# A SwiGLU's last down projection: three pairs in seven products, pair by pair through four banks, none plainly

## The chip, the cores and the metric

One core of a Trainium2 chip runs the whole kernel. TensorE (PE in the profile) multiplies matrices into PSUM banks, VectorE (DVE) and ScalarE (ACT) do the elementwise work, GpSimd (POOL) adds a few small operations and accumulating DMAs, SyncE (SP) issues most DMAs. The metric is the device time of one execution in microseconds. Three runs of the kernel before gave 2554.17, 2554.62 and 2554.91; the median, 2554.62, stands as its time.

## The reference

Two groups of tokens (512 and 256) go through two layers with shared weights. Each layer is a half SwiGLU, a mixer, and a half SwiGLU, all on a residual stream of width 1024; a final RMSNorm ends it. Everything is float32.

```python
def swiglu(h, wg, wu, wd):
    return (jax.nn.silu(h @ wg) * (h @ wu)) @ wd

def even_layer(x, ...):
    x = x + 0.5 * swiglu(rmsnorm(x, f1_n), f1_g, f1_u, f1_d)
    x = x + mixer_ab(rmsnorm(x, mix_n), w_in, ...)
    x = x + 0.5 * swiglu(rmsnorm(x, f2_n), f2_g, f2_u, f2_d)
    return x

def odd_layer(x, ...):
    x = x + 0.5 * swiglu(rmsnorm(x, f1_n), f1_g, f1_u, f1_d)
    x = x + mixer_c(rmsnorm(x, mix_n), w_qkv, rpb, w_out)
    x = x + 0.5 * swiglu(rmsnorm(x, f2_n), f2_g, f2_u, f2_d)
    return x
```

`wg` and `wu` are 1024 x 2816, `wd` is 2816 x 1024. So there are four SwiGLUs. What follows them is, in order: the first mixer, the next layer's SwiGLU, the second mixer, and the end of the kernel.

## The kernel before

**Layout.** The residual stream lies transposed: `x[m]`, m = 0 to 7, holds 128 of the 1024 features for all 768 tokens. The tokens are cut into two halves of 384 (`H`), the free size of nearly every matmul.

**Precision.** A float32 product is made of three fp32r products. Each operand is split into a high part (a copy by ACT) and a low part (source minus high part, by DVE); `mm3` issues high x high, high x low, low x high. `wsplit` splits a 128 x 512 weight tile into `whi` and `wlo`, which come from a pool of five places each; `split` does it for operands of 384 columns.

**Seven products.** The hidden width 2816 is eleven *pairs* (`NPAIR`) of two blocks of 128. For one pair, the down projection is a 2 x 2 block product: two hidden blocks, two halves of the outputs (features of m < 4 and of m >= 4), two halves of the tokens. A scheme of Strassen's kind makes it in seven block products instead of eight. The weight operands are three of the four blocks (`a11`, `a12`, `a22`) and the sums `s1` (of two blocks), `s3` (of two blocks), `s2` = `s1` + `a11`, `s4` = `s2` + `a12`. `s1` and `s3` are built by DMA: SP loads one block, POOL issues a second DMA that accumulates onto it (`wsum`); `s2` and `s4` are DVE adds (`sums`). The operand side has `b11`, `b21`, `t1`, `t2`, `t3`, `b22`, `n4`, each a split of a hidden tile or of a difference of such tiles (`operands`, a generator that is stepped by hand). A block product covers four 128-feature blocks j, each in a PSUM bank of its own. Banks carry names: X gets b11 then b21; Y starts as a copy of X after b11 and gets t2, t3, n4; Z gets t1 then b22. Between products a bank's content is added to, or subtracted from, `x` where the scheme wants it (`add`), and `out` does the last such add for a row and then calls `final`.

**The order of pairs.** `ffn` makes gate and up projections pair by pair, with the down projection of pairs 0 to 7 two at a time in between (`down`). The last three pairs, 8, 9 and 10, come in `down_last`. There, pairs 8 and 9 go together in seven products, and pair 10, whose hidden tiles are ready last, goes *plainly*: its two blocks are two more weight tiles per output half (`quads`, split by `lasts`), and its operands are just the split hidden tiles (`operand`), four block products for each hidden block. For each j, `part` does both pairs' matmuls one after the other into the bank, then `plain` adds pair 10's.

**What follows decides the order in `down_last`.** `lag` is true before another SwiGLU and at the end, false before a mixer. With `lag`: b11, t2, b21, t3, then X finished plainly, n4 with Y finished plainly, `half_done(0)` (the norm of token half 0 may begin), t1, the plain product of the other half in a bank V, b22 finished plainly, `half_done(1)`. Without: b11, t2, b21, X finished plainly, t1, b22 finished plainly, t3, copies of Y into four further banks W, then for each j n4 and the two plain products. At the end of the kernel the last block is cut into columns (`CUTS`: 256 and 128) so that the final norm of the first part may start early.

**What `final` does** for a row m: its squares (ACT) are summed into `acc` (DVE); before a SwiGLU the row is fed into that SwiGLU's operands (`feed`); before a mixer, when the row's second half is done, the row is scaled by the norm's gain and split into `xh[m]` (ACT) and `xl[m]` (DVE), on which the mixer's first projection waits. Before the first mixer this goes in two halves of 384 columns; before the second the tokens are turned, and the parts are 448, 64 and 256 columns, so that the first spans both halves. The mixer's first projection goes through m = 0 to 7 in order.

**Order on the engines.** The program fixes the order on PE (with small matmuls of the norm put in by an own count of PE's time, `tick`). On the other engines and the DMA queues a scheduler orders the instructions when the program is built: those listed earlier go first among the ones that its model holds ready, and a later one may go ahead while an earlier one isn't. Tiles of a tag share a fixed number of places: 8 raw weight tiles (`raw`), 8 tiles for sums (`s`), 30 operand tiles of 384 columns (`e`), 5 places for `whi` and `wlo`, four PSUM banks in each of two pools (`mm`, `aux`).

## Time and profile before

| what | value |
|---|---|
| median of three runs | 2554.62 us |
| the profiled execution | 2555.03 us |
| its span in the profile | 2553.3 us |
| PE, PEld busy | 99%, 97% |
| DVE, ACT, POOL busy | 82%, 54%, 13% |
| the four runs of `down_last` (start to end on PE) | 452.30 to 498.74; 1179.08 to 1225.87; 1663.71 to 1711.13; 2494.55 to about 2544.2 |

In the profile, PE is the matmul, PEld the weight load beside it, an instruction's row names its start, its length, its engine and source line, and output <- inputs. Almost every matmul has line 191 (inside `mmul`), so stages are told apart by tile names: `db`, `dt`, `dn` are the operands b11/b21/b22, t1/t2/t3 and n4 of the paired products, `dh` those of pair 10's plain ones, `whi`/`wlo` (or `khi`/`klo`) the weights, `ps_mm` and `ps_aux` the banks, `xh`/`xl` a mixer's operands. On DVE, line 877 and 879 are `add` for m < 4 and m >= 4, 281 the norm's sum, 993 `xl`, 168 `wlo`, 745 `sums`. Idle time of an engine stands in brackets with what ended it.

### The profile page before, as it was taken

How to read it: one execution, taken by the hardware profiler on the slowest of the kernel's cores; microseconds unless marked ns; L12 is line 12 of the kernel's file. 1: busy time of each engine (PE TensorE's matmuls, PEld its weight loads, DVE VectorE, ACT ScalarE, POOL GpSimd, SP SyncE). 2: the span in 40 equal slices, each digit the busy share in tenths (PEclk: the TensorE clock that was granted, in tenths of full speed). 3: DMA queues.
4: the chain of work that ended last, by engine and by line, in shares of the span. 5: the costliest groups of instructions: out<-in, count | busy, mean ns of one | idle time of the engine just before them, and what ended most of it. 6: DMA issues, size and time to landing. Idle time of an engine off the chain costs nothing.

```text
span 2553.3 us, 42563 instructions
## 1 busy us (share of the span) xinstructions
PE 2535.2 (99%) x15160; PEld 2475.6 (97%) x15160; DVE 2092.9 (82%) x4206; ACT 1369.3 (54%) x2844; POOL 322.7 (13%) x398
## 2 busy tenths in 40 slices
PE   9999999999999999999999999999999999999998
PEld 8999999988899999999999999999999999999998
DVE  8987888888879778888988788876667598878887
ACT  7554455546665545445654445554455475444553
POOL 1110111000111111110111011112112111101100
PEclk9999999999999999999999999999999999999999
DMA  8654555431256455552665455432212256545451
GB/s 235 159 133 120 131 134 148 145 98 62 73 146 175 120 126 127 131 131 79 161 153 132 117 127 125 121 124 70 63 61 65 88 148 164 135 119 126 123 125 54
DMA packets 187156, 310.88 MB, mean 122 GB/s; under 512 B 31680, under 2 KB 46528, under 8 KB 186944
## 3 DMA queue, kind: packets, MB, share of 16 engines
q1 hardware_dynamic: 149248, 240.49, 29.4%
q0 software_dynamic: 36864, 67.13, 16.7%
q8 instruction: 119, 1.95, 0.3%
q14 instruction: 93, 0.76, 0.1%
q10 hardware_dynamic: 832, 0.55, 0.1%
HBM read 298.65 MB, written 15.07 MB: 123 GB/s over the span
## 4 chain that ended last, share of the span: by engine, by line
PE 92%; DVE 4%; ACT 1%; issue 1%; DMA 1%; POOL 0%; SPq 0%; ACTq 0%; DVEq 0%; POOLq 0%
PE ps_mm L191 60%; PE ps_aux L191 30%; PE ps_aux L202 1%; DVE wlo L168 1%; DMA s<-in_w 1%; DVE ol L255 0%; DMA raw<-in_w 0%; DVE u L587 0%; DVE s L745 0%; ACT whi L167 0%; DMA x<-in_x 0%; ACT xh L992 0%; DVE db L255 0%; DVE dt L255 0%; DVE tl L255 0%
## 5 line engine op out<-in xcount | busy, mean ns | idle before, releaser
L167 ACT CAST whi<-s 128x512 fp32r<-128x512 f32 x508 | 310.6, 620 | 384.3 <-PE ps_mm L191 198.6
L168 DVE TENSOR_TENSOR wlo<-s,whi 128x512 fp32r<-128x512 f32 x508 | 345.3, 687 | 173.6 <-ACT whi L167 152.0
L148 POOL DMA_DIRECT2D s<-in_w x256 | 223.5, 911 | 1442.0 <-DVE db L255 356.7
L167 ACT CAST whi<-rawp 128x512 fp32r<-128x512 f32 x344 | 211.4, 619 | 255.5 <-PE ps_mm L191 100.7
L168 DVE TENSOR_TENSOR wlo<-rawp,whi 128x512 fp32r<-128x512 f32 x344 | 234.4, 686 | 23.4 <-ACT whi L167 14.4
L191 PE MATMUL ps_mm<-db,whi 128*128 128x384 f32 (+1 forms) x948 | 240.2, 334 | 0.0
L191 PE MATMUL ps_aux<-dt,whi 128*128 128x384 f32 x880 | 223.3, 334 | 0.0
L191 PEld LDWEIGHTS ps_mm<-db,whi 128*128 128x128 f32 x948 | 170.8, 188 | 0.0
L191 PE MATMUL ps_mm<-db,wlo 128*128 128x384 f32 (+1 forms) x474 | 158.4, 334 | 0.7 <-DVE wlo L168 0.7
L191 PEld LDWEIGHTS ps_aux<-dt,whi 128*128 128x128 f32 x880 | 158.8, 188 | 0.0
L191 PE MATMUL ps_aux<-dt,wlo 128*128 128x384 f32 x440 | 147.2, 334 | 0.3 <-DVE wlo L168 0.3
L191 PE MATMUL ps_mm<-xh,whi 128*128 128x512 f32 (+1 forms) x416 | 144.4, 347 | 0.0
L167 ACT CAST whi<-raw 128x512 fp32r<-128x512 f32 x164 | 100.4, 619 | 79.6 <-PE ps_mm L191 56.9
L191 PE MATMUL ps_mm<-xl,whi 128*128 128x512 f32 (+1 forms) x416 | 140.2, 337 | 0.0
L191 PE MATMUL ps_mm<-xh,wlo 128*128 128x512 f32 (+1 forms) x416 | 140.1, 337 | 0.0
L168 DVE TENSOR_TENSOR wlo<-raw,whi 128x512 fp32r<-128x512 f32 x146 | 99.0, 687 | 27.2 <-ACT whi L167 25.1
L587 DVE TENSOR_TENSOR u<-ps_aux,u 128x384 f32<-128x384 f32 x176 | 97.3, 553 | 7.6 <-PE ps_aux L191 7.4
L1190 ACT ACTIVATE p<-p,st 128x256 f32<-128x256 f32 (+3 forms) x144 | 69.1, 481 | 54.9 <-DVE st L1185 54.8
L191 PEld LDWEIGHTS ps_mm<-db,wlo 128*128 128x128 f32 x474 | 89.0, 188 | 1.5 <-DVE wlo L168 1.5
L191 PEld LDWEIGHTS ps_mm<-xh,whi 128*128 128x128 f32 x416 | 78.9, 190 | 9.4 <-issue 1.2
L191 PEld LDWEIGHTS ps_mm<-xh,wlo 128*128 128x128 f32 x416 | 78.8, 189 | 8.6
L191 PEld LDWEIGHTS ps_mm<-xl,whi 128*128 128x128 f32 x416 | 79.0, 190 | 6.7
(508 smaller groups left out, 8028.2 us busy)
## 6 DMA issues: line engine op xcount, KB each, us to landing
rawp<-in_w SPq DMA_DIRECT2D x384, 256.0 KB, 3.1
s<-in_w SPq DMA_DIRECT2D x256, 256.0 KB, 2.8
s<-in_w POOLq DMA_DIRECT2D x256, 256.0 KB, 5.0
raw<-in_w SPq DMA_DIRECT2D x163, 256.0 KB, 2.9
xdm<-x SPq DMA_DIRECT2D x16, 384.0 KB, 2.3
x<-in_x SPq DMA_DIRECT2D x16, 192.0 KB, 4.8
x<-xdm SPq DMA_DIRECT2D x8, 384.0 KB, 3.8
tab<-skew SPq DMA_DIRECT2D x8, 256.0 KB, 3.6
```

The lines of the kernel that those rows point to most:

```text
L148: self.nc.gpsimd.dma_start(f, y, accum_op=ALU.add)
L167: i = nc.scalar.copy(hi, src).ins
L168: self.behind = i, (eng or nc.gpsimd).tensor_tensor(out=lo, in0=src, in1=hi.bitcast(F32), op=ALU.subtract).ins
L191: self.nc.tensor.matmul(out, lhsT=lhsT, rhs=rhs, start=start, stop=stop, **kw)
L202: self.nc.tensor.transpose(out, src, self.ident)
L587: nc.vector.tensor_tensor(out=t, in0=bank[key, n], in1=t, op=ALU.add)
L1190: nc.scalar.activation(outs[i - n0], outs[i - n0], AF.Exp, scale=-1.0, bias=mn[:, i : i + 1], accum_out=sm[:, i : i + 1])
```

## The change

`down_last` takes pairs 8, 9 and 10 together, all in seven products, and nothing goes plainly: `quads`, `operand`, `plain` and `lasts` go, and the second copy of Y into W.

- A product now goes *pair by pair*: the weight tile of pair 8 is split and its matmuls run through the four banks j = 0 to 3, then pair 9's, then pair 10's. What follows a bank (an add, `out`, a copy) follows pair 10's matmuls in it. Before, the two pairs alternated within each bank.
- Pair 10's operands come from the same generator as those of the others (`own`), stepped between the products.
- `s2` of pair 10 is written in place over its `a11` tile; the eight places for sums hold three `s1`, three `s3` and two `s2`.
- The order is the same for all four stages up to the fifth product: b11, b21 with `out` of rows 0 to 3 of token half 0, t2, t1, t3. Then, before a mixer, b22 and n4; otherwise n4, `half_done(0)`, b22. Before a mixer, `below` finishes rows 4 to 7 in both halves after the n4 product.
- At the end of the kernel, `ending` splits the three `s4` tiles first and does b22 bank by bank with the same column cuts.
- `wsplit` loses the variants for tiles kept in the `s` tag and for a negative sign.

```diff
@@ ffn
-        self.down_last(pre, range(NPAIR - 3, NPAIR - 1), d, hs[NPAIR - 1])
+        self.down_last(pre, range(NPAIR - 3, NPAIR), d, operands(NPAIR - 1))
@@ sums
-            t = s[n, "s2"] = self.fw.tile([P, 4, P], F32, tag="s", name=name, bufs=8)
+            t = s[n, "s2"] = a11 if n == NPAIR - 1 else self.fw.tile([P, 4, P], F32, tag="s", name=name, bufs=8)
@@ down_last
...
+        def part(st, p, b, key, j, start, cols=slice(0, H)):
+            self.mm3(
+                bank[key, j][:, cols], (st[0][:, j, :], st[1][:, j, :]), [t[:, cols] for t in d[p][b]],
+                start and p == pairs[0], p == pairs[-1], not start,
+            )
+
+        def product(w, b, key, start, then):
             for p in pairs:
-                self.mm3(
-                    bank[key, j][:, cols], (st[p][0][:, j, :], st[p][1][:, j, :]), [t[:, cols] for t in d[p][b]],
-                    start and p == pairs[0], stop and p == pairs[-1], not (start and stop),
-                )
-
-        def plain(st, half, key, j, cols=slice(0, H)):
...
+                st = self.wsplit(w[p], nc.vector)
+                for j in range(4):
+                    if start and p == pairs[0]:
+                        bank[key, j] = self.psum()[:, :H]
+                    part(st, p, b, key, j, start)
+                    if p == pairs[-1]:
+                        then(j)
...
+        def below(j):
+            out(4 + j, 0, "Y")
             if not lag:
+                self.final(4 + j, H, T)
+
+        def ending():
+            st = {p: self.wsplit(s4[p], nc.vector) for p in pairs}
+            for js, cuts in ((0, 1), ((0, H),)), ((2, 3), CUTS):
                 for a, b in cuts:
                     for j in js:
-                        part(st, "b22", "Z", j, False, cols=slice(a, b))
-                        plain(u, 1, "Z", j, slice(a, b))
-                        out(j, 1, "Z", a, b, ends and j == 3)
+                        for p in pairs:
+                            part(st[p], p, "b22", "Z", j, False, slice(a, b))
+                        out(j, 1, "Z", a, b, j == 3)
...
+        more(own, 4)
+        product(w["a11"], "b11", "X", True, seed)
+        more(own, 2)
+        s2 = sums("s2")
+        product(w["a12"], "b21", "X", False, lambda j: out(j, 0, "X"))
+        more(self.later, 3)
+        product(s2, "t2", "Y", False, lambda j: add(j, 1, bank["Y", j]))
+        more(own, 5)
+        s4 = sums("s4")
+        product(sums("s1"), "t1", "Z", True, lambda j: add(4 + j, 1, bank["Z", j]))
+        product(sums("s3"), "t3", "Y", False, lambda j: (out if lag else lambda m, h, k: add(m, h, bank[k, j]))(4 + j, 1, "Y"))
+        if not lag:
+            product(s4, "b22", "Z", False, lambda j: out(j, 1, "Z"))
+        product(w["a22"], "n4", "Y", False, below)
         if lag:
...
             self.half_done(0)
...
+            if ends:
+                ending()
+            else:
+                product(s4, "b22", "Z", False, lambda j: out(j, 1, "Z"))
                 self.half_done(1)
```

More of the change, by code (lines that the diff above doesn't have):

```diff
@@ L830, in steps_last, with down_last @@
             yield next(rest)
-    def down_last(self, pre, pairs, d, h):
+    def down_last(self, pre, pairs, d, own):
         nc = self.nc
         lag = self.following[0] in ("f", "last")
-        last = NPAIR - 1
-        s, bank, dl = {}, {}, {}
-        def quads(p):
-            q = [self.region(f"{pre}_w_down", 2 * p + k, 1, 0, D) for k in (0, 1)]
-            return self.parts(*[r[:, i * 512 : (i + 1) * 512] for i in (0, 1) for r in q])
+        ends = self.following[0] == "last"
+        s, bank = {}, {}
@@ L842, in down_last, with more @@
         w = self.down_parts(pre, pairs, s)
         sums = lambda name: {p: self.sums(w["a11"][p], w["a12"][p], s, p, name) for p in pairs}
-        split = lambda w: {p: self.wsplit(w[p], nc.vector) for p in pairs}
         view = lambda m, half: self.x[m][:, HALVES[half][0] : HALVES[half][1]]
-        def more(n):
+        def more(gen, n):
             for _ in range(n):
-                next(self.later, None)
-        def operand(i, half):
-            dl[i, half] = self.dtile("h"), self.dtile("h")
-            self.split(*dl[i, half], h.pop((i, half)))
@@ L855, in part @@
[L855 to L872 removed]
+                next(gen, None)
@@ L887, in out @@
                 self.final(m, half * H + a, half * H + b)
-        def seed(to, key, j):
-            bank[to, j] = (self.psum(self.aux, "aux") if to == "Y" else self.psum())[:, :H]
-            nc.scalar.copy(bank[to, j], bank[key, j])
-        def lasts(i):
-            return [self.wsplit(quads_last[2 * i + k], nc.vector, lag and i == 0, -1 if i else 1) for k in (0, 1)]
-        s2 = sums("s2")
-        st = split(w["a11"])
-        s3 = sums("s3")
-        for j in range(4):
-            part(st, "b11", "X", j, True)
-            seed("Y", "X", j)
@@ L902, in down_last @@
-        quads_last = quads(last)
-        st = split(s2)
-        for j in range(4):
-            part(st, "t2", "Y", j, False)
-            add(j, 1, bank["Y", j])
-        s4 = sums("s4")
-        st = split(w["a12"])
-        for j in range(4):
-            part(st, "b21", "X", j, False)
-        operand(0, 0)
-        operand(1, 0)
-        def seventh():
-            st = split(s3) if lag else {p: s3[p, "split"] for p in pairs}
-            for j in range(4):
-                part(st, "t3", "Y", j, False)
-                if lag:
-                    add(4 + j, 1, bank["Y", j])
@@ L921, in fifth, with seed @@
-        def fifth():
-            st = split(sums("s1"))
-            for j in range(4):
-                part(st, "t1", "Z", j, True)
-                add(4 + j, 1, bank["Z", j])
-        def third(u):
-            st = {p: self.wsplit(s4[p], nc.vector, lag and p == pairs[1]) for p in pairs}
+        def seed(j):
+            bank["Y", j] = self.psum(self.aux, "aux")[:, :H]
+            nc.scalar.copy(bank["Y", j], bank["X", j])
+        def below(j):
+            out(4 + j, 0, "Y")
             if not lag:
-                s3.update({(p, "split"): self.wsplit(s3[p], nc.vector, p == pairs[1]) for p in pairs})
-            ends = self.following[0] == "last"
-            for js, cuts in (((0, 1), ((0, H),)), ((2, 3), CUTS)) if ends else ((range(4), ((0, H),)),):
+                self.final(4 + j, H, T)
@@ L938, in third @@
                     if cuts is CUTS:
                         self.spawn(self.finish(1, H + a, H + b))
-        if lag:
-            seventh()
-        more(3)
-        u = lasts(0)
-        for j in range(4):
-            plain(u, 0, "X", j)
-            out(j, 0, "X")
-        operand(0, 1)
-        operand(1, 1)
-        if lag:
-            st = split(w["a22"])
-            v = lasts(1)
-            for j in range(4):
-                part(st, "n4", "Y", j, False)
-                plain(v, 0, "Y", j)
-                out(4 + j, 0, "Y")
-            self.half_done(0)
-            fifth()
-            for j in range(4):
-                plain(v, 1, "V", j)
-                out(4 + j, 1, "V")
-            third(u)
-            if self.following[0] != "last":
-                self.half_done(1)
-        else:
-            fifth()
-            third(lasts(0))
-            seventh()
-            for j in range(4):
-                seed("W", "Y", j)
-            st = split(w["a22"])
-            v = lasts(1)
-            for j in range(4):
-                part(st, "n4", "Y", j, False)
-                plain(v, 0, "Y", j)
-                out(4 + j, 0, "Y")
-                plain(v, 1, "W", j)
-                out(4 + j, 1, "W")
```

26 lines of the change are left out of this document (3 added, 23 removed).

## The prediction

> **What bounds the kernel now.** I read the page's shares and chain first, then the chain piece by piece, then busy time by stage, then single instructions at the ends of the stages.
>
> ```profile
> span 2553.3 us, 42563 instructions
> PE 2535.2 (99%) x15160; PEld 2475.6 (97%) x15160; DVE 2092.9 (82%) x4206; ACT 1369.3 (54%) x2844; POOL 322.7 (13%) x398
> ...
> PE 92%; DVE 4%; ACT 1%; issue 1%; DMA 1%; POOL 0%; SPq 0%; ACTq 0%; DVEq 0%; POOLq 0%
> ...
> 394.22 16.64 PE ps_mm L191 x96
> ```
>
> PE is 92% of the chain, so a matmul fewer is time saved where nothing else is late. The last row is a chain piece without a wait: 96 matmuls of 384 columns in 16.64 us, **0.1733 us each** (their spacing; they overlap).
>
> The last down projection runs four times: before the first mixer, before the second SwiGLU of a pair, before the second mixer, and at the end (two rows). Columns: length; busy and count of PE, PEld, DVE, ACT, POOL; clock; DMA share; GB/s.
>
> ```profile
> 452.30:498.74 46.44, 46.16 (x265) 45.67 (x265) 39.27 (x75) 29.02 (x59) 0.00 (x0) 1.00 0.38 124
> 1179.08:1225.87 46.79, 46.79 (x274) 46.75 (x274) 41.48 (x80) 30.82 (x64) 1.24 (x1) 1.00 0.20 63
> 1225.87:1262.00 36.13, 36.13 (x213) 36.09 (x213) 33.46 (x64) 23.23 (x50) 8.03 (x9) 1.00 0.73 174
> 1663.71:1711.13 47.42, 46.72 (x266) 45.64 (x266) 39.64 (x80) 30.09 (x66) 0.00 (x0) 1.00 0.31 109
> 2494.55:2533.46 38.91, 38.74 (x227) 38.38 (x226) 29.11 (x55) 17.00 (x34) 0.88 (x1) 1.00 0.00 1
> 2533.46:2544.50 11.04, 10.71 (x81) 10.57 (x80) 9.03 (x21) 3.30 (x8) 0.69 (x1) 1.00 0.39 144
> ...
> 1685.91 0.44 PE L191 MATMUL ps_mm<-db,wlo 128*128 128x384 f32 x1 [0.38 <-DVE wlo L168]
> ...
> 1700.44 0.45 PE L191 MATMUL ps_aux<-dh,wlo 128*128 128x384 f32 x1
> ...
> 2526.60 0.83 PE L191 MATMUL ps_aux<-ones,acc 128*128 128x1 f32 x6 [0.17 <-DVE acc L281]
> ```
>
> Before, a stage has 7 products x 4 banks x 2 pairs x 3 = 168 matmuls and 96 plain ones: 264, or 45.75 us. The two stages before mixers take 46.44 and 47.42, so **0.69 and 1.67 us are waits** of PE; the rows at 1685.91 and 1700.44 are two places where the longer one loses it (weight splits that come late). DVE is busy 85% and 84% of those two stages: it is the second bound.
>
> **The change part by part.** *Matmuls.* 7 x 4 x 3 x 3 = 252 per stage, 12 fewer, 2.08 us; four stages: **-8.3 us**.
>
> *Weight splits.* 18 or 20 per stage become 21, but a split now feeds 12 consecutive matmuls (2.08 us) instead of sharing 24 with its partner, and the pool holds five. So a split may be made up to four blocks, 8.3 us, ahead. I let the waits of 0.69 and 1.67 go: **-2.4**, and in the last stage 38.91 less 37.44 for 216 matmuls and about 0.9 for the norm's small ones (the row at 2526.60 and three transposes): **-0.6**. Bounds: none of it, to all 3.0. What is late next is the other work of DVE.
>
> *New DVE work.* Rows around the second mixer's start show what an operation occupies, from its start to the next start.
>
> ```profile
> 1711.13 0.39 PE L191 MATMUL ps_mm<-xh,whi 128*128 128x512 f32 x1
> ...
> 1712.01 0.55 DVE L879 TENSOR_TENSOR x<-x,ps_aux 128x384 f32<-128x384 f32 x1
> 1712.47 0.55 DVE L879 TENSOR_TENSOR x<-x,ps_mm 128x384 f32<-128x384 f32 x1
> 1712.94 0.69 DVE L168 TENSOR_TENSOR wlo<-raw,whi 128x512 fp32r<-128x512 f32 x1
> 1713.54 1.02 DVE L281 TENSOR_TENSOR acc<-acc,sq 128x384 f32<-128x384 f32 x2
> 1714.47 1.27 DVE L993 SCALAR_TENSOR_TENSOR xl<-x,gains,xh 128x448 fp32r<-128x448 f32 x3
> 1715.66 0.42 DVE L1499 CAST mb<-mf 128x512 bf16<-128x512 f32 x1
> ...
> 1716.15 0.39 PE L191 MATMUL ps_mm<-xl,whi 128*128 128x512 f32 x1
> ```
>
> An add or norm sum of 384 takes 0.47 us, a split of 512 0.60, the three low parts of a row 1.19. Per stage the third pair adds 3 operand splits and 4 differences (3.3 us), 2 sums (1.2) and 1 split (0.6): **5.1 us of DVE** in a stage 2 to 4 us shorter, where DVE had 7.2 and 7.8 us idle. It fits, but hardly; inside the stage I price it at nothing beyond what follows, with 0 to 2 us per stage as bounds.
>
> *Ends of the stages before mixers.* Here the change moves most. Before, the last block finishes a bank pair each 3.1 us (18 matmuls), so DVE takes a row as it comes. Even so it ends late: PE starts the projection at 1711.13, the last row's low part ends at 1715.74, and PE reads that row at 1716.15, **0.4 us later**. After, the last pair's pass finishes four banks 0.52 us apart, in the sixth product (rows 0 to 3) and 6.24 us later in the seventh (rows 4 to 7, whose other half is finished there too). Let E be PE's end of the stage; the sixth product's first bank is ready at E-7.8 (6.24 + 1.56). From there at the earliest, second mixer: rows 0 to 3 cost 4 adds, 3 sums, 4 x 1.19 = 8.05; rows 4 to 7 cost 4 adds, 8 sums and 4 x 1.19 = 10.4, of which 2.3 depend on one half only and could go earlier. DVE ends at E+8.3 to E+10.7; the row is due at E+5.0; a split of the projection's own weights (0.6) may lie between. **PE waits 3.3 to 6.3 us; I take 5.3**, the upper part, because DVE comes to these rows with hardly a pause. Bounds: 0, if the order on DVE leaves the norm's sums for later, and 10.
>
> First mixer: parts go by halves, so early ones can leave early. This is seen before, too: the low parts at 475.00 run ahead of the add at 476.06, though the program lists them behind such an add.
>
> ```profile
> 475.00 1.15 DVE L993 SCALAR_TENSOR_TENSOR xl<-x,gains,xh 128x384 fp32r<-128x384 f32 x2
> 476.06 0.56 DVE L877 TENSOR_TENSOR x<-ps_mm,x 128x384 f32<-128x384 f32 x1
> ...
> 498.74 0.39 PE L191 MATMUL ps_mm<-xh,whi 128*128 128x512 f32 x1
> ...
> 504.80 0.49 PE L191 MATMUL ps_mm<-xh,whi 128*128 128x512 f32 x1
> ```
>
> A half row costs 0.53. Rows 0 to 3: 1.88 + 1.41 + 2.12 = 5.4; rows 4 to 7: 5.64 + 2.1 to 4.2. DVE ends at E+5.4 to E+7.5; the last row is due at 504.80, E+6.1 (the norm's small matmuls go before it here). **Wait 0 to 2 with a weight split between; I take 1.5**, bounds 0 and 6.
>
> *Before a SwiGLU.* No operand is due soon: the latest, t2, is split by 1234.73 and read at 1250.83.
>
> ```profile
> 1234.18 0.55 DVE L255 TENSOR_TENSOR t23l<-tmp,t23h 128x384 fp32r<-128x384 f32 x1
> ...
> 1250.83 0.33 PE L191 MATMUL ps_mm<-t20h,whi 128*128 128x384 f32 x1
> ```
>
> Sixteen us of cover take some 8 us more of backlog, though DVE stays 93% busy until 1262; **+0.3**, bounds 0 and 2.
>
> *End.* Half 0 of the output was written behind three blocks of matmuls:
>
> ```profile
> 2523.66 0.33 PE L191 MATMUL ps_mm<-dt,whi 128*128 128x384 f32 x1
> ...
> 2530.50 0.49 PE L202 MATMUL ps_aux<-ident,sm 128*128 128x128 f32 x3
> ...
> 2532.04 2.18 DVE L325 SCALAR_TENSOR_TENSOR y<-x,gains,ps_aux 128x384 f32<-128x384 f32 x4
> ...
> 2544.54 0.43 PE L202 MATMUL ps_aux<-ident,sm 128*128 128x128 f32 x2 [0.37 <-DVE x L877]
> ...
> 2545.41 2.44 DVE L325 SCALAR_TENSOR_TENSOR y<-x,gains,ps_aux 128x256 f32<-128x256 f32 x6 [0.91 <-ACT acc L1017]
> ...
> 2548.24 1.64 DVE L325 SCALAR_TENSOR_TENSOR y<-x,gains,ps_aux 128x128 f32<-128x128 f32 x6 [0.39 <-ACT acc L1017]
> ...
> 2550.29 0.40 ACTq L1038 DMA_DIRECT2D out_y<-y  x1
> ...
> 2549.00:2550.00 1.00, 0.00 (x0) 0.00 (x0) 0.88 (x4) 0.32 (x2) 0.15 (x1) 0.50 1.08 381
> ```
>
> After, only a seventh of a stage (6.2 us of matmuls, and the norm's own) is left behind half 0, whose norm took 6.8 us before (2523.66 to 2530.50). PE's last matmul before was through by 2544.17; with 2.1 + 0.6 us taken off it is at about 2541.5. Half 0's norm is then ready about 1 us earlier, at 2540.5, and its eight scalings (2.18 us for four) hold DVE until 2544.8, the six of 256 columns until 2546.9, and the last six, which could start at 2548.24 - 2.7 = 2545.5, come 1.4 us late. Half 0's 1.57 MB also go through DMA just ahead of half 1's; the last row shows DMA full at 381 GB/s, 4.1 us for them, which fits. **+1.4**, bounds 0 and 3.
>
> *Loads.* 21 tiles a stage for 18, two of the three more by an accumulating DMA of POOL, which is 13% busy:
>
> ```profile
> rawp<-in_w SPq DMA_DIRECT2D x384, 256.0 KB, 3.1
> ...
> s<-in_w POOLq DMA_DIRECT2D x256, 256.0 KB, 5.0
> ```
>
> The ninth raw tile waits for the first pair's place and is used in the sixth or seventh product, over 25 us later; nothing of the stage stands behind it on SP that is due before the fifth. Nothing, then; without that cover a load costs its 3.1 to 5.0 us from issue to landing (last column).
>
> **Sum:** -8.3 - 2.4 - 0.6 + 5.3 + 1.5 + 0.3 + 1.4 = -2.8. The profiled execution took 2555.03 (span 2553.3), 0.41 above the median 2554.62; so 2552.2 in its own terms and **2551.8** as a median.
>
> **The rivals.** *The backlog hides.* If DVE's order fills every gap, the rows come at the early ends or before: waits 0 and 1.5, tail 0.5. -11.3 + 2.0 = -9.3: **2545.3**. For it: early parts are taken in advance at 475.00. Against: 85% and 84% busy before 5.1 us are added.
>
> *Slower: the projection's first weights queue behind the rows.* Their split stands after all finals in the program. If it isn't issued before E-7.8, DVE reaches it after the rows, at about E+6.3 and E+10, and PE stands from its first matmul. It decides whether that one split goes early. -11.3 + 6.3 + 10 + 1.7 = +6.7: **2561.3**. Against: of five places in the pool, its own is free when the sixth product's second pair is through, at E-8.3, just in time.
>
> *The clock drops in that wait.* At the end of the run the granted clock falls after PE goes quiet:
>
> ```profile
> 2545.00:2546.00 1.00, 0.34 (x3) 0.26 (x3) 0.58 (x2) 0.54 (x2) 0.54 (x1) 1.00 0.00 0
> 2546.00:2547.00 1.00, 0.00 (x0) 0.00 (x0) 1.00 (x4) 0.60 (x2) 1.00 (x3) 0.96 0.00 0
> 2547.00:2548.00 1.00, 0.47 (x1) 0.18 (x1) 0.85 (x3) 0.47 (x2) 0.38 (x1) 0.50 0.74 261
> ```
>
> From 1.00 to 0.50 within two us. The projection's first 24 matmuls (22 of them lie between 1711.13 and 1716.15: 5.5 us for all) would take twice that: up to 11 more in both mixers, **2572**. [...]
>
> *The products starve.* DVE saturated inside the stages, 0.8 us a stage, 3.2 on top of my sum: **2555.0**, and the change seems to do nothing.
>
> **How the numbers follow.** This kernel's measurement tells about 0.2%, 5.1 us, from no change: faster is below 2549.5, slower above 2559.7. Chances: forecast 0.40 (2547 to 2556, 0.07 of it below 2549.5), backlog hidden 0.32, starving 0.10, slower 0.10, clock 0.04, something else 0.04 (half of it slower). Faster 0.39, same 0.45, slower 0.16. The range runs from just under the hidden case, **2544.5**, to the slower one, **2561.5**; the forecast's own is 2547 to 2556.
>
> **What would show it.** Right: 252 matmuls a stage, stages before mixers near 43.7 us; then rows of xh and xl at 4 to 7 of the first projection with PE waiting on DVE, longer in the second mixer; half 0's scalings beside half 1's. Wrong: no such waits (hidden), a wait ahead of the projection's first matmul (slower), a clock under 1.00 there, or waits on wlo inside the stages (starving). Most likely wrong in my sum are the two mixer waits, since the order on DVE isn't known.

## The result, and the profile after

After the change the kernel takes 2567.59 us (median of 6 runs, 2566.02 to 2572.42); the kernel before, run beside it, 2554.39 (6 runs, 2554.05 to 2555.36). The ratio is **1.0053, with a 95% interval of 1.0043 to 1.0064**: 13 us slower, outside the predicted range, where 2.8 us faster was forecast. The profiled execution took 2566.82 us.

The page after the change: span, busy times, and the chain's shares. Source lines have moved: in this kernel 182 is `mmul`, 159 `wlo`, 272 the norm's sum, 856 and 858 `add`, 922 and 923 `xh` and `xl`; in e12 to e16 `mmul` is 202.

```profile
span 2565.0 us, 42558 instructions
...
PE 2531.9 (99%) x15106; PEld 2470.1 (96%) x15106; DVE 2109.3 (82%) x4242; ACT 1374.7 (54%) x2856; POOL 330.4 (13%) x406
...
PE 91%; DVE 5%; ACT 2%; DMA 1%; issue 1%; POOL 0%; SPq 0%; ACTq 0%; DVEq 0%; POOLq 0%
```

The page hardly differs. PE is busy 3.3 us less than before (2535.2), in a span 11.7 us longer: the matmuls went, and waits came. Where they came shows in the windows of the stages and of what follows each (columns as in the prediction).

```profile
451.34:495.02 43.68, 43.68 (x254) 43.68 (x254) 41.73 (x81) 27.53 (x55) 0.00 (x0) 1.00 0.35 105
495.02:502.08 7.06, 5.26 (x23) 3.68 (x22) 7.06 (x15) 5.70 (x13) 0.00 (x0) 1.00 0.92 326
1177.69:1223.06 45.37, 44.01 (x253) 43.46 (x252) 40.18 (x77) 29.90 (x62) 0.00 (x0) 1.00 0.25 81
1223.06:1256.00 32.94, 28.30 (x154) 27.59 (x154) 30.59 (x60) 20.09 (x43) 4.70 (x5) 0.95 0.42 100
1668.87:1712.55 43.68, 43.68 (x253) 43.68 (x253) 39.40 (x82) 26.91 (x59) 0.00 (x0) 1.00 0.27 91
1712.55:1728.03 15.48, 9.04 (x29) 6.48 (x29) 12.65 (x25) 8.81 (x20) 5.62 (x5) 0.78 0.64 214
```

The stages ahead of the mixers take 43.68 us without a wait, as predicted (46.44 and 47.42 before). The loss lies **behind** them: from the first matmul of the second mixer's projection to the norm's matmuls 15.48 us, 6.16 before (1711.13 to 1717.29), with 9.04 of PE's work and a granted clock of 0.78. In the second row DVE is busy all 7.06 us while PE waits 1.80.

PE's waits over the whole kernel (total, times, longest), the largest that are new:

```profile
PE ps_mm L182 <- DVE wlo L159: 7.9, 7, 5.0
PE ps_aux L182 <- DVE acc L272: 3.8, 3, 1.7
PE ps_mm L182 <- DVE x L856: 2.4, 1, 2.4
```

And single instructions, before and in the SwiGLU (1198 to 1240) and before mixer 1:

```profile
1198.29 0.44 PE L182 MATMUL ps_mm<-dt,wlo 128*128 128x384 f32 x1 [1.36 <-DVE wlo L159]
...
1224.31 0.69 DVE L159 TENSOR_TENSOR wlo<-raw,whi 128x512 fp32r<-128x512 f32 x1
1224.91 1.02 DVE L856 TENSOR_TENSOR x<-ps_mm,x 128x384 f32<-128x384 f32 x2
...
1225.61 0.66 PE L182 MATMUL ps_mm<-b110h,whi 128*128 128x384 f32 x1 [2.38 <-DVE x L856]
1226.07 0.52 PE L182 MATMUL ps_mm<-b110l,whi 128*128 128x384 f32 x1
1226.38 0.52 PE L182 MATMUL ps_mm<-b110h,wlo 128*128 128x384 f32 x1
...
1235.96 0.41 PE L182 MATMUL ps_mm<-b110h,whi 128*128 128x384 f32 x1 [1.34 <-ACT t22h L245]
...
1239.23 0.44 PE L182 MATMUL ps_mm<-b210h,whi 128*128 128x384 f32 x1 [0.91 <-ACT p L610]
...
1716.24 0.50 PE L182 MATMUL ps_mm<-xh,whi 128*128 128x512 f32 x1 [0.76 <-ACT xh L922]
1717.25 1.02 DVE L272 TENSOR_TENSOR acc<-acc,sq 128x384 f32<-128x384 f32 x2
1717.39 0.50 PE L182 MATMUL ps_mm<-xl,whi 128*128 128x512 f32 x1 [0.64 <-DVE xl L923]
1718.19 0.68 DVE L923 SCALAR_TENSOR_TENSOR xl<-x,gains,xh 128x448 fp32r<-128x448 f32 x1
1718.79 1.02 DVE L272 TENSOR_TENSOR acc<-acc,sq 128x384 f32<-128x384 f32 x2
...
1721.26 0.68 DVE L923 SCALAR_TENSOR_TENSOR xl<-x,gains,xh 128x448 fp32r<-128x448 f32 x1
1721.85 0.42 DVE L1429 CAST mb<-mf 128x512 bf16<-128x512 f32 x1
1722.19 1.28 DVE L159 TENSOR_TENSOR wlo<-raw,whi 128x512 fp32r<-128x512 f32 x2
1722.92 0.80 PE L182 MATMUL ps_mm<-xh,wlo 128*128 128x512 f32 x1 [5.03 <-DVE wlo L159]
1723.52 0.63 PE L182 MATMUL ps_mm<-xh,whi 128*128 128x512 f32 x1
1723.94 0.63 PE L182 MATMUL ps_mm<-xl,whi 128*128 128x512 f32 x1
```

Before mixer 1, DVE alternates rows and pairs of norm sums (0.60 and 0.94 us) until 1721.85; the split of the projection's second weight tile (k = 4 to 7) stands behind them all, so PE, which has used row 4 since 1716.24, stands until 1722.92, though row 5 is ready at 1718.9 (the end of the `xl` at 1718.19). Before the SwiGLU, its first product needs a PSUM bank that the last product has just filled; the add that frees it is at 1224.91, behind weight splits, feeds and sums of DVE. Behind both waits matmuls come at 1.8 times their spacing: 0.42 us apart instead of 0.23 (1723.52 to 1723.94), and 0.31 instead of 0.17 (1226.07 to 1226.38). The windows around the second wait show why (the eighth column is the clock):

```profile
1718.00:1720.00 2.00, 0.00 (x0) 0.00 (x0) 2.00 (x5) 2.00 (x5) 0.00 (x0) 1.00 0.98 288
1720.00:1722.00 2.00, 0.00 (x0) 0.00 (x0) 2.00 (x5) 0.98 (x4) 0.00 (x0) 0.61 0.03 8
1722.00:1724.00 2.00, 1.08 (x3) 0.89 (x4) 2.00 (x5) 0.38 (x2) 1.59 (x1) 0.50 0.33 84
1724.00:1726.00 2.00, 2.00 (x6) 1.60 (x5) 1.39 (x3) 0.00 (x0) 2.00 (x2) 0.50 0.91 278
1726.00:1728.00 2.00, 2.00 (x7) 1.55 (x6) 0.00 (x0) 0.00 (x0) 2.00 (x4) 0.68 0.81 278
```

What PE loses by this I count as (1 - clock) x its busy time, summed over such windows: 0.5 x 1.08 + 0.5 x 2.00 + 0.32 x 2.00 = 2.2 us here, 1.5 before the SwiGLU. In the kernel before, the same count gives 0.1 us in all, at its very end.

### The profile page after: what moved, and what is told of

The parts are those of the page before. It is cut to its first block, busy times and chain, and to the rows that moved or that the text cites. A ratio compares the mean times of both kernels' runs of the same rounds, so it can differ in the third digit from the quotient of the medians.

```text
span 2565.0 us, 42558 instructions
## 1 busy us (share of the span) xinstructions
PE 2531.9 (99%) x15106; PEld 2470.1 (96%) x15106; DVE 2109.3 (82%) x4242; ACT 1374.7 (54%) x2856; POOL 330.4 (13%) x406
## 4 chain that ended last, share of the span: by engine, by line
PE 91%; DVE 5%; ACT 2%; DMA 1%; issue 1%; POOL 0%; SPq 0%; ACTq 0%; DVEq 0%; POOLq 0%
PE ps_mm L182 59%; PE ps_aux L182 30%; PE ps_aux L193 1%; DVE wlo L159 1%; DMA s<-in_w 1%; DMA raw<-in_w 0%; ACT whi L158 0%; DVE acc L272 0%; DVE ol L246 0%; DVE s L736 0%; DVE u L578 0%; DVE y L316 0%; DVE db L246 0%; DMA x<-in_x 0%; DVE dt L246 0%
## 5 line engine op out<-in xcount | busy, mean ns | idle before, releaser
L158 ACT CAST whi<-rawp 128x512 fp32r<-128x512 f32 x356 | 219.0, 619 | 268.3 <-issue 102.5
L182 PE MATMUL ps_mm<-db,whi 128*128 128x384 f32 (+1 forms) x1068 | 269.2, 333 | 0.0
L159 DVE TENSOR_TENSOR wlo<-rawp,whi 128x512 fp32r<-128x512 f32 x356 | 242.5, 685 | 27.1 <-ACT whi L158 15.1
L182 PE MATMUL ps_aux<-dt,whi 128*128 128x384 f32 x960 | 243.5, 334 | 0.0
L182 PEld LDWEIGHTS ps_mm<-db,whi 128*128 128x128 f32 x1068 | 192.2, 188 | 0.0
L182 PE MATMUL ps_mm<-db,wlo 128*128 128x384 f32 (+2 forms) x534 | 177.7, 333 | 0.0
L182 PEld LDWEIGHTS ps_aux<-dt,whi 128*128 128x128 f32 x960 | 173.3, 188 | 0.0
L182 PE MATMUL ps_aux<-dt,wlo 128*128 128x384 f32 x480 | 160.5, 334 | 0.3 <-DVE wlo L159 0.3
L182 PEld LDWEIGHTS ps_mm<-db,wlo 128*128 128x128 f32 x534 | 100.3, 188 | 0.0
L182 PEld LDWEIGHTS ps_aux<-dt,wlo 128*128 128x128 f32 x480 | 90.1, 188 | 1.0 <-DVE wlo L159 1.0
L182 PEld LDWEIGHTS ps_mm<-xh,whi 128*128 128x128 f32 x416 | 79.5, 191 | 10.7 <-issue 1.2
```

Source lines behind the costliest of these rows:

```text
L158: i = nc.scalar.copy(hi, src).ins
L159: self.behind = i, (eng or nc.gpsimd).tensor_tensor(out=lo, in0=src, in1=hi.bitcast(F32), op=ALU.subtract).ins
L182: self.nc.tensor.matmul(out, lhsT=lhsT, rhs=rhs, start=start, stop=stop, **kw)
```

## The experiments

The table divides each profile at the first matmuls of the four `down_last` stages: m0 from the first to the second, f to the third, m1 to the fourth, end to the span's end. In brackets what half clock cost in that part, counted as above (for the end it is left out). A profile is one execution; medians are of all.

| run | median, us | m0 | f | m1 | end |
|---|---|---|---|---|---|
| before | 2554.4 | 726.78 | 484.63 | 830.84 | 58.75 |
| after | 2567.6 | 726.35 | 491.18 (1.5) | 836.43 (2.2) | 59.70 |
| e1_old_f | 2563.3 | 727.85 (1.7) | 484.63 | 836.43 (2.3) | 60.52 |
| e2_f_adds | 2572.1 | 727.91 (1.7) | 494.33 (4.8) | 836.40 (2.2) | 59.64 |
| e3_m_early | 2573.4 | 729.54 (3.4) | 492.63 (3.4) | 837.91 (4.9) | 59.68 |
| e4_banks_all | 2563.8 | 725.18 | 490.34 (1.7) | 833.83 (1.7) | 59.91 |
| e5_pool1 | 2575.1 | 730.40 (3.3) | 492.99 | 837.01 (1.5) | 60.28 |
| e6_pool2 | 2578.2 | 734.00 (3.4) | 489.74 | 838.55 (1.7) | 61.45 |
| e7_banks_pool | 2575.0 | 733.21 (5.0) | 494.35 (3.1) | 834.86 (1.6) | 60.39 |
| e8_warm | 2570.3 | 729.47 (3.4) | 489.63 | 837.97 (1.7) | 59.85 |
| e9_no_sums | 2567.7 | 727.90 (1.7) | 488.24 | 836.58 (2.6) | 59.89 |
| e10_banks_end | 2569.5 | 728.43 (1.7) | 489.30 (1.4) | 839.58 (2.3) | 59.29 |
| e11_load | 2557.7 | 727.41 | 485.83 | 832.29 | 58.76 |
| e12_end_work | 2557.9 | 724.86 | 484.63 | 836.46 (5.0) | 58.83 |
| e13_end_work_pairs | 2560.7 | 727.56 (1.7) | 484.63 | 837.67 (6.3) | 58.81 |
| e14_end_no_first | 2566.8 | 731.73 (2.3) | 484.63 | 837.76 (1.4) | 58.58 |
| e15_halves | 2552.6 | 724.80 | 484.62 | 830.81 | 58.54 |
| e16_halves_both | 2552.4 | 724.82 | 484.62 | 830.61 | 58.87 |

After minus before: -0.43 in m0, +6.55 in f, +5.59 in m1, +0.95 at the end, and -0.96 ahead of the first stage, in code that the change leaves alone: +11.7.

### Undoing one stage

```diff
-        self.down_last(pre, range(NPAIR - 3, NPAIR), d, operands(NPAIR - 1))
+        if kind in ("f",):
+            self.down_last_old(pre, range(NPAIR - 3, NPAIR - 1), d, hs[NPAIR - 1])
+        else:
+            self.down_last(pre, range(NPAIR - 3, NPAIR), d, operands(NPAIR - 1))
```

> The down projection ahead of a SwiGLU is as before the change; ahead of the two mixers and at the end it stays changed. Theory (the loss sits at the stage borders, each by itself, and the one ahead of the SwiGLU is the largest): the marks of the two traces give +6.56 us between the start of that stage and the first t2 product of the next SwiGLU, so the time falls from 2567.6 to about 2561, and the other stages keep their marks (m1 +5.6, last +1.0, m0 -0.4). Rival (a loss of the whole kernel, as by more work on VectorE in every stage or a lower clock throughout): the time falls by a quarter of the 13 us lost or less, to 2564 or above.

2563.3 (ratio to before 1.0037, 1.0023 to 1.0051). Part f is back at 484.63 to the hundredth, and m1 and the end keep their loss: each stage loses by itself, as the theory has it. The time falls by 4.3 instead of 6.6, and the profile shows 1.7 of the rest: mixer 0 runs at half clock for a while, in code that is the same as in the changed kernel, whose own profile has no drop there. So that drop comes in some executions only. This fits the spread of the changed kernel's six runs, 6.4 us for 1.3 before the change: the mean granted clock was 0.996 in the three shortest, 0.995 in the next two and 0.994 in the longest.

### Moving one instruction forward on VectorE

```diff
 # e2: the adds that free b22's banks, before a SwiGLU
-            add(m, half, bank[key, m % 4], a, b)
+            with self.tc.high_priority() if self.following[0] == "f" and key == "Z" else nullcontext(): add(m, half, bank[key, m % 4], a, b)
 # e3: the split of a mixer's first weight
-            hi, lo = self.wsplit(part, self.nc.vector)
+            with self.tc.high_priority() if first else nullcontext():
+                hi, lo = self.wsplit(part, self.nc.vector)
```

> Only the order on VectorE ahead of the SwiGLU changes: the four adds that free the PSUM banks of b22 go ahead of the weight splits and feeds of the next SwiGLU. Theory (the bank is late because its add stands in a queue): the 2.38 us wait of the first b11 matmul goes, the clock behind it stays at 1.00 instead of 0.95, and the feeds come about 2 us later, which the first product of 4 us mostly covers: 2564 to 2566. Rival (VectorE has too much to do there in whatever order): the wait moves to the feeds b212, b213 and the time stays at 2567 to 2568.5.

> Only the split of the first projection's weights in the two mixers is put ahead of the rows: on VectorE one subtraction of 0.55 us in each mixer moves from behind the rows of k = 0 to 3 to ahead of them. Theory (the second weight tile is late because it stands behind all rows): ahead of mixer 1 the wait of 5.03 us for that split goes, and waits for the rows of k = 4 to 7 take its place, 1.5 us or less each, during which TensorE does 9 to 12 matmuls that now follow the wait; the clock does not drop to 0.5: 2563.5 to 2565.5. Rival (the rows alone hold the projection, the weights only come with them): the last row ends 0.55 us later than now and the time stays within 1 us of 2567.6.

Both are slower than the change: 2572.1 and 2573.4. In e2 the 2.38 us wait is gone, but the norm's matmuls now wait 2.4 us for their sum and b21 2.8 for a PSUM bank, and the clock falls twice; f without the clock's 4.8 is 489.5, without its 1.5 in the changed kernel 489.7. So the order of that queue only chose which matmul waits. In e3 the long wait is gone too: no wait ahead of mixer 1 exceeds 1.4 us. But they are many, and the clock falls for longer; windows of e3:

```profile
1722.00:1724.00 2.00, 1.13 (x4) 0.48 (x3) 2.00 (x5) 2.00 (x5) 0.00 (x0) 1.00 0.88 351
1724.00:1726.00 2.00, 1.40 (x5) 0.78 (x5) 2.00 (x5) 0.35 (x1) 0.00 (x0) 1.00 0.21 55
1726.00:1728.00 2.00, 0.68 (x3) 0.19 (x1) 2.00 (x5) 1.61 (x4) 1.55 (x1) 1.00 0.62 197
1728.00:1730.00 2.00, 1.20 (x4) 0.90 (x4) 2.00 (x2) 0.90 (x3) 2.00 (x3) 0.76 0.73 246
1730.00:1732.00 2.00, 2.00 (x9) 1.71 (x8) 2.00 (x3) 0.00 (x0) 1.82 (x2) 0.50 0.32 86
```

PE never stands for a whole window, DVE is busy in every one, and the clock still goes to 0.50. Neither theory had that.

### The clock by itself

```diff
...
+            if ps: self.proj(ws[0], xs, GROUPS[0], ps[0], range(4), True, False), self.junk(ps[1], 24)
...
+        if pre == "l1_ffn1": self.warm(11)
```

> Like the changed kernel, but TensorE does work without use in two of the waits: 24 matmuls of 512 columns (about 5.2 us) between the rows k = 3 and k = 4 of the first projection of mixer 1, and 11 (2.4 us) ahead of the SwiGLU's first product. Nothing else moves. The waits stay as long as they were; only the clock can gain. Theory (part of the loss is the halved clock behind the waits, 2.2 and 1.5 us in the profile of the changed kernel): granted clock 1.00 in both places, 2563.5 to 2565. Rival (the half-rate rows cost nothing, since VectorE is what they wait for anyway): 2567 to 2568.

2570.3: no gain in the median. Where the matmuls without use were put (the 24 took 5.5 us, 1717.03 to 1722.50), the clock stayed at 1.00, and f is 1.55 us shorter, the 1.5 that were counted; to the norm's matmuls mixer 1 needs 13.46 us instead of 15.48. But mixer 1 gave it back: it then waited 1.97 us for the norm's power on POOL, and the clock fell there (1.7). And mixer 0 lost 3.4 us in this profile, none in that of the changed kernel. The price of a drop is shown; filling two of the waits isn't a cure.

### How much work, or when

```diff
 # e9: s2 and s4 of the last three pairs left out
-        sums = lambda name: {p: self.sums(w["a11"][p], w["a12"][p], s, p, name) for p in pairs}
+        sums = lambda name: {p: s[p, "s1" if name in ("s2", "s4") else name] for p in pairs}
 # e11: the kernel before, with work without use on VectorE behind each split
+            for lo in [st[k][1].bitcast(F32) for k in (st if isinstance(st, dict) else (0, 1))]:
+                nc.vector.tensor_tensor(out=self.pad, in0=self.pad, in1=lo[:, 0:2, :], op=ALU.max)
```

> Like the changed kernel, but the second sum s2 and the fourth s4 of the three last pairs' weights are left out of the last down projection: the products t2 and b22 take the tile s1 in their place (the output is not the reference's). Six operations of 128x512 fewer on VectorE in each stage, 0.60 us each, 3.6 in all; matmuls, splits and their order in the program are the same, and no other engine gets more. Theory (VectorE's amount of work): the waits behind the stages shrink by 2 to 3.6 us each in three places and with them some of the clock drops: 2556 to 2562. Rival (order and bunching alone): 2565 to 2568, with the 5.03 us wait ahead of mixer 1 as it was.

> The kernel before the change, with work without use on VectorE: after each weight split of the last down projection a maximum of 128x256, 19 a stage, about 0.35 us each, 6 to 7 us a stage; nothing else. The change adds 5.1 us of VectorE a stage by the count of its operations. Theory (amount of work on VectorE): waits behind the stages and clock drops appear in the old order of matmuls too, and the time rises from 2554.6 to 2562 to 2575. Rival (the order of the new products, their banks 0.52 us apart): VectorE had 7.2 and 7.8 us idle in the two stages that were measured, which takes the work: 2554 to 2558.

These two decide against the amount of work, ahead of the mixers at least. First a stage of e9 with its wait behind it, then a stage of e11:

```profile
1669.23:1712.91 43.68, 43.68 (x253) 43.68 (x253) 37.17 (x77) 27.04 (x59) 0.00 (x0) 1.00 0.25 83
1712.91:1728.74 15.83, 9.39 (x28) 6.75 (x28) 12.63 (x25) 8.81 (x20) 5.97 (x6) 0.78 0.63 215
```

```profile
1664.55:1712.38 47.83, 46.85 (x266) 45.57 (x265) 44.41 (x95) 29.69 (x64) 0.00 (x0) 1.00 0.29 100
```

In e9 DVE idles 6.5 us in the stage instead of 4.3, and 15.83 us follow as 15.48 did: 2567.7, as slow as the change. Only f gains, some 1.4 us beside the clock. In e11 DVE is 93% busy in that stage, more than after the change (90%), and the kernel takes 2557.7 (1.0003 to 1.0022): 3 us. So ahead of the mixers the DVE work in the stage's middle isn't the point. That leaves what **becomes ready only with the last banks and is due at once**. e4 and e10 change that by having each bank's matmuls of the three pairs in a row, so that banks end 1.56 us apart:

```diff
+            if True:          # e10: if b in ("n4", "b22"):
+                st = {p: self.wsplit(w[p], nc.vector) for p in pairs}
+                for j in range(4):
+                    if start:
+                        bank[key, j] = self.psum()[:, :H]
+                    for p in pairs:
+                        part(st[p], p, b, key, j, start)
+                    then(j)
+                return
```

> The seven products stay in their order, but each goes bank by bank again: the three pairs' tiles are split first, then each of the four banks takes its 9 matmuls, so that a product's banks end 1.56 us apart instead of 0.52. Theory (the bunching of the last product's banks fills VectorE at the stage's end): the work left on VectorE at the end of the stage falls by about two adds and their rows, 2 to 3 us, and the time falls to 2561 to 2565, less 1 to 2 us for waits on three splits at the start of products. Rival (VectorE's whole work, or the order of the products, b22 and n4 last): 2567 or slower, with the same waits at the borders.

> Like the changed kernel, but the two last products of a stage, n4 and b22, go bank by bank (three tiles split first, then each bank 9 matmuls); the five ahead of them stay pair by pair. With all seven bank by bank the time was 2563.75, of which waits for splits inside the stages were 0.3, 2.6 and 1.1 us by the windows. Theory (bunching at the very end is what counts, the rest of the products only pays for it): the gain at the ends stays and these waits go by half: 2560 to 2563. Rival (the gain of that run came from spreading all evacuations, the fifth and sixth products' too): 2564 to 2567.

2563.8 and 2569.5. All seven products that way win 1.2 us in m0 and 2.6 in m1, as the theory of bunching had it; the last two alone, which should have been the cheaper half, lose 2.1 and 3.2 us there and win 1.9 in f. Before mixer 1 the weight split came so late that PE waited 9.20 us for it in one piece, in place of 5.03:

```profile
1725.37 0.79 PE L182 MATMUL ps_mm<-xh,wlo 128*128 128x512 f32 x1 [9.20 <-DVE wlo L159]
```

### Work moved to POOL

```diff
-                st = self.wsplit(w[p], nc.vector)
+                st = self.wsplit(w[p], nc.gpsimd if p == pairs[1] and b != "b11" else nc.vector)
```

> Like the changed kernel, but in the second to seventh product the low half of the middle pair's weight split is computed on POOL instead of VectorE: six subtractions a stage, of about 0.60 us on VectorE and 1.30 on POOL (the mean of POOL's own weight splits elsewhere). Theory (VectorE's amount of work at the stages' ends is the bound, and an order only moves the wait): about 3.6 us a stage leave VectorE; the waits behind the stages, some 5.5 ahead of mixer 1, 4.6 ahead of the SwiGLU and 1.8 ahead of mixer 0, shrink by 2 to 3 us each and the clock drops behind them go with them: 2556 to 2562. Rival (the bunching of the banks, not the amount): 2566 to 2568. Rival (POOL slows VectorE, or its splits come late): waits for wlo inside the stages, 2568 or slower.

> The same with two of the three pairs' splits on POOL, twelve a stage. Theory (amount of work): 7.2 us a stage leave VectorE, waits and clock drops behind the stages are nearly gone: 2550 to 2557, unless POOL, with 2.6 us of splits in each 6.2 us product, becomes late itself. Rival (bunching): no better than with six. Rival (POOL disturbs VectorE): slower than with six.

> Bank by bank as in the run before (2563.75) and with the middle pair's splits on POOL. Theory (amount): 2 to 3 us less at each of three stage ends, less a little for POOL's later splits at the starts of the products, where all three tiles are needed at once: 2556 to 2561. If bunching and amount were one and the same cost, there is no more to gain than by the better of the two: 2560 to 2564.

All three are slower than their counterpart: 2575.1, 2578.2, 2575.0. In the first stage of e5 DVE has 75 operations instead of 81 and is busy as long (41.94 us, 41.73). Two rows that show where the gain went:

```profile
1675.49 1.29 POOL L159 TENSOR_TENSOR wlo<-rawp,whi 128x512 fp32r<-128x512 f32 x1 [9.74 <-ACT whi L158]
1675.78 1.41 DVE L589 TENSOR_TENSOR u<-u,acc 128x384 f32<-128x384 f32 x1
```

The DVE operation, 0.55 us elsewhere, began beside POOL's, took 1.41 us and ended 0.4 us after it. In that first stage four of DVE's operations are stretched like this beside POOL's six, by 3.9 us together (an estimate, against the median length of their kind in the trace); the six subtractions taken off DVE come to 3.6.

### The work at the stage's end taken away

Now only the two stages ahead of the mixers are as changed. e12 does n4 and b22 bank by bank, makes the norm sums of rows 4 to 7 for the second half after t3, where they are ready, and puts the projection's weight split ahead (e3's edit). e13 is without the bank order, e14 without the split's place.

```diff
...
-        product(sums("s3"), "t3", "Y", False, lambda j: (out if lag else lambda m, h, k: add(m, h, bank[k, j]))(4 + j, 1, "Y"))
+        product(sums("s3"), "t3", "Y", False, lambda j: (out if lag else lambda m, h, k: (add(m, h, bank[k, j]), self.norm_add(m, H, T)))(4 + j, 1, "Y"))
...
```

> The change in the two stages ahead of the mixers only (the ones ahead of the SwiGLU and at the end as before), with three edits that take work off the moment at which TensorE leaves the stage: n4 and b22 go bank by bank, so that their banks end 1.56 us apart; the norm sums of rows 4 to 7 for the second half of the tokens, which are ready after t3, are added there and not behind n4; the projection's first weight splits go ahead of the rows. Theory (what counts is the work on VectorE that becomes ready only at the stage's end and is due at once): TensorE's waits behind the two stages fall under 1 us each, no clock drop follows them, and each stage keeps its 2.1 us of matmuls and part of the old waits inside: 2548.5 to 2551.5. Rival (the new order of pairs or products costs in the stage itself, or the work only moves on): 2553 to 2558. Rival (VectorE's total amount): as slow as the changed kernel in these stages, 2558 to 2562.

> The same without the bank order: all seven products pair by pair, as the change has them, with the sums made early and the projection's weights first; only in the two stages ahead of the mixers. Behind n4 four adds, four sums of the first half and four rows' low parts remain due at once on VectorE, 0.47 + 0.47 + 1.19 us each in mixer 1 (8.5 in all, against 10.4 before) and 0.47 + 0.47 + 0.53 in mixer 0 (5.9). Theory: mixer 0 waits for under 1 us, mixer 1 for 2 to 4 us, with or without a clock drop: 2551 to 2556. If the bank order is worth nothing: the same time as the run before.

> As the first of these three (bank by bank at the end, sums early), but the projection's weight splits stand where the list of priorities puts them, behind the rows. Theory (one late split of 0.6 us decides over a whole wait when it stands behind all rows): ahead of mixer 1 a wait for the second weight tile of 2 to 5 us comes back, and a clock drop behind it: 2552 to 2558. Rival (with the rows spread, the split's place doesn't matter): within 1 us of the first of these three.

e12: 2557.9 (0.9998 to 1.0016). Part m0 is 1.9 us shorter than before the change; m1 isn't, with 5.0 us of half clock in it. That drop doesn't come each time: of e12's eleven runs, five took 2553.9 to 2556.2 us with a mean granted clock of 0.998 or 0.999, and six, the profiled one among them, 2557.9 to 2558.8 with 0.996. e14: 2566.8, and the two waits for the split stand there alone:

```profile
501.56 0.79 PE L202 MATMUL ps_mm<-xh,wlo 128*128 128x512 f32 x1 [4.98 <-DVE wlo L159]
...
1721.76 0.80 PE L202 MATMUL ps_mm<-xh,wlo 128*128 128x512 f32 x1 [7.49 <-DVE wlo L159]
```

The place of one subtraction of 0.6 us in each mixer is worth 8.8 us in all when the rows that it stands behind are no longer the bound; in e3, where the rows were late as well, the clock took more than it gained. e13 (2560.7) puts the bank order at 2.8 us, the clock's part included.

What is left in e12 is the clock, with short waits ahead of it:

```profile
1712.31 0.50 PE L202 MATMUL ps_mm<-xh,whi 128*128 128x512 f32 x1 [1.30 <-ACT xh L1101]
1713.25 0.50 PE L202 MATMUL ps_mm<-xl,whi 128*128 128x512 f32 x1 [0.44 <-DVE xl L1102]
...
1714.52 0.52 PE L202 MATMUL ps_mm<-xl,whi 128*128 128x512 f32 x1 [0.28 <-DVE xl L1102]
```

e15 gives PE other matmuls there: it takes k = 0 to 3 of the first weight for both groups of tokens before k = 4 to 7 of either. e16 does so for both first weights, whose splits both go ahead of the rows. In both, the norm's matmuls come 3 us later in the plan (the first pair of lines).

```diff
-        yield DELAYM[0]
+        yield DELAYM[0] + 3.0 * cols
...
-            todo = [(g, which, self.proj(ws[which], xs, GROUPS[g])) for g in (0, 1) for which in (0, 1)] if pr == 0 else []
+            todo = [(g, which, self.psum()) for g in (0, 1) for which in (0, 1)] if pr == 0 else []
+            for n in ((0,), (1,)) if todo else ():
+                for ks in (range(4), range(4, KD)):
+                    for g, which, ps in todo:
+                        if which in n:
+                            self.proj(ws[which], xs, GROUPS[g], ps, ks, ks[0] == 0, ks[0] > 0)
```

> The first run of the last three (the change ahead of the mixers only, bank by bank at the end, sums early, projection's weights first), and in mixer 1 the first weight's projection takes k = 0 to 3 of both groups of tokens before k = 4 to 7 of either: 12 matmuls of 256 columns, 1.4 us, come between the rows that are ready and those that are not; the norm's matmuls come 3 us later in the plan. VectorE's order is the same. There the waits of TensorE ahead of mixer 1 were 1.3 + 0.4 + 0.3 us between 1710.3 and 1714.5, and the clock stood at 0.5 for 10 us behind them, 5.0 us lost. Theory (the rest of the loss is the clock, and it takes less than 2 us of waits scattered over 4 us to lose it): waits below 0.7 us, no drop, 2551 to 2553.5. Rival (rows stay late by as much, the wait only moves): 2556 to 2558.5.

> The same with both first weights (k = 0 to 3 of two weights and both groups of tokens, 8.4 us of matmuls, before any row from 4 on); the split of the second weight's two tiles goes ahead of the last rows too, 1.2 us more on VectorE there. Theory: no wait at all ahead of mixer 1, no drop: 2550 to 2553, no faster than the run before by more than 1 us if that one has no drop. Rival (the two splits delay the rows by as much as the order hides): 2553 to 2558.

First the windows of e12 that include the drop, then the same place in e15:

```profile
1712.00:1714.00 2.00, 1.25 (x4) 0.67 (x4) 2.00 (x5) 1.61 (x4) 0.00 (x0) 1.00 0.95 358
1714.00:1716.00 2.00, 1.72 (x5) 1.09 (x5) 2.00 (x6) 0.27 (x1) 0.67 (x1) 0.71 0.24 69
1716.00:1718.00 2.00, 2.00 (x10) 1.90 (x9) 1.23 (x3) 0.00 (x0) 2.00 (x2) 0.50 0.75 235
1718.00:1720.00 2.00, 2.00 (x9) 1.81 (x9) 0.54 (x1) 0.18 (x1) 2.00 (x4) 0.50 0.81 254
```

```profile
1712.00:1714.00 2.00, 1.55 (x5) 0.67 (x4) 2.00 (x5) 1.75 (x4) 0.00 (x0) 1.00 0.93 336
1714.00:1716.00 2.00, 1.74 (x12) 1.65 (x13) 2.00 (x6) 0.01 (x1) 0.92 (x1) 1.00 0.17 42
1716.00:1718.00 2.00, 2.00 (x14) 1.74 (x13) 2.00 (x5) 0.62 (x1) 2.00 (x1) 1.00 0.82 253
```

With three waits of 0.2 to 0.3 us left, the clock stays, and 2552.6 is 5.3 us below e12, which counted 5.0 us of drop. All eleven runs of e15 have a clock of 0.998 or 0.999; against the five such runs of e12 (median 2554.4) the gain is 1.8 us, so most of the 5.3 is the drop. e16, with no wait at all there, is at 2552.4. Both beat the changed kernel by 15 us and lie 2 us below the kernel before beside them (2554.6), by a ratio of 0.9992 with an interval of 0.9983 to 1.0001: no difference that this settles. In the profile, mixer 0's part is 2.0 us shorter than before the change. Mixer 1's comes out even: its stage, with n4 and b22 bank by bank, takes 45.4 us, of which 1.2 is a wait; it took 47.4 before the change and 43.7 pair by pair. The stage before the SwiGLU and the one at the end are the old ones in e12 to e16, so no run shows a cure for the change's loss there.

## Why the prediction was wrong

Part by part, the forecast was -1.3 in m0, -1.8 in f, +1.6 in m1 and -1.3 at the end; the profile has -0.4, +6.6, +5.6 and +1.0. More than half of the miss lies in f.

- *Matmuls, -8.3, and waits inside the stages, -2.4:* right before the mixers (43.68 us, no wait). Before the SwiGLU a new one of 1.36 came (1198.29).
- *Before mixer 1, +5.3 with bounds 0 and 10:* waits of 6.4 us (15.48 less 9.04), 2.2 of half clock behind them, 9.3 in all with what else lies there. The rows and sums on DVE were rightly counted (last row at E+9.4 for E+8.3 to E+10.7). What the sum lacked is the weight split: the rival put it ahead of the first matmul, and it was the second tile that stood behind the rows. Its place decides (e14), once the rows don't (e3). So the kind of wait was right, its size too small, and the clock behind it was missing.
- *Before mixer 0, +1.5:* right in size, 1.8 us of waits, in part by luck: 1.40 of it is for the norm's sum (502.08) and only 0.40 for a row, where the forecast had the last row. It wasn't foreseen that they cost another 1.7 to 3.4 of half clock in some executions.
- ***Before a SwiGLU, +0.3 with bounds 0 and 2: the step that failed most.*** 8.6 us went there: +6.55 with the 2.1 of matmuls not gained. "No operand is due soon" asked only for operands. What was due soon was a PSUM bank that the next SwiGLU's first product takes over, and which an `add` of DVE frees late (2.38). The 0.91 at 1239.23 is for a bank that ACT must copy out. The 1.34 at 1235.96 ends as one more such add (1235.27 to 1235.82) and ACT's split `t22h` end, and which of the two the matmul needed isn't settled. With the 1.36 inside the stage these are all 6.0 us that PE stands in part f (none before the change); with 1.5 of clock they make 7.5 of the 8.6, and the rest wasn't traced. Why DVE is late there is shown in part only: its amount of work was worth 1.4 us (e9), the bank order 1.8 (e10), both without the clock, and moving the adds ahead nothing (e2). "DVE stays 93% busy until 1262" stood in the same sentence and should have widened the bound: the old kernel had 0.2 us of slack on DVE in the 25 us behind that stage.
- *End, +1.4:* cost 3.6 (+0.95, with 2.1 + 0.6 not gained), over its bound of 3; waits of 0.73, 1.70 and 0.54 for the norm's sums. No experiment bears on it.
- *The clock:* the sum held nothing for it. That three matmuls per row in the wait keep the clock up was an assumption that no run had shown, and this is the reasoning that fell: e3 and e12 lose the clock with no wait over 1.4 us. It cost the profile 3.7 us besides the end, and up to 12 in other orders.
- *Starving inside the stages* didn't happen before the mixers (43.68 us, no wait), and *too much work on VectorE* explains little there: e9 wins nothing in m0 and m1, e11 loses 0.6 and 1.5 us in them.

So the change takes 2 us a stage off PE and gives them back, several times over, at the stages' ends. Ahead of the mixers the cause is shown: the three pairs' last pass closes four banks within 1.56 us of the stage's end, and what hangs on these banks is on DVE, ahead of a weight split, when PE comes for it; spreading the banks, making sums early and moving the split take most of the loss away, other matmuls in the last waits the rest (e12 to e16). Before the SwiGLU, the largest loss, the waits are shown and the same cause is argued; at the end it stays open.

## What to carry to other kernels

When an edit regroups the last pass over several accumulators, count what becomes ready with each of them and when it is due, on every engine and for every resource that the next stage takes over (PSUM banks and weight tiles as well as operands), rather than the total work of the stage. An engine that is 90% busy over a stage can be the bound for the 10 us that follow it (DVE before mixer 1: 90%, and 6.4 us of PE's waits behind it). Price a wait of TensorE by what it does to the clock as well: here some 2 us of short waits close together cost more than their sum in six runs of eleven, and other matmuls put in their place were worth 5 us in the median.

## What the runs showed of the hardware

- **The clock fell without a long wait.** In e12, waits of 1.3, 0.4 and 0.3 us between 1710.6 and 1714.5 were followed by about 10 us at 0.50; in e15 0.2 + 0.2 + 0.3 by none. The length alone doesn't decide: in e16 a single wait of 1.8 us (for `sm` of POOL, between 1720 and 1724) was followed by no drop, with 1.00 in every window to 1740, while the longest ahead of e12's drop was 1.3. Of the 31 sums in brackets in the table, 14 are 1.4 to 1.7 us and 6 are 3.1 to 3.4.
- **Whether it fell differed between executions.** Mixer 0 behind its 1.8 us of waits ran at full clock in one profile of the changed kernel, and lost 1.7 us in e2's, whose program is the same up to there. The eleven runs of e12 fall into five without and six with the lower mean clock, some 4 us apart.
- **It didn't always come back at once.** In e12 PE was busy from 1716 on, and the clock stayed at 0.50 until about 1725, in further windows like the last two shown.
- **DVE operations beside one of POOL took longer, not all of them.** In e5 those at 1675.78, 1684.01 and 1690.09, each begun 0.3 to 0.4 us after a split of POOL, took 1.41, 1.34 and 1.33 us for 0.55 and ended 0.4 us after it; four adds from PSUM banks at 1694.56, beside POOL's split at 1694.70, took 1.93 us together, as without one (1.94 at 1705.70). POOL relieved DVE of nothing in the first stage: 41.94 us busy with six operations fewer, 41.73 with them.
